# Memory operands beside the state space output, memory tiles ahead of the rows, and the second keys in two halves

## The chip, the cores and the metric

One core of one Trainium2 chip. The metric is device time of one execution in microseconds. Three runs of the kernel before gave 1411.87, 1414.42 and 1416.46 us, a median of 1414.42.

## What is computed

One layer of a streaming encoder on 1024 frames of width 1024, in fp32: token mixing (an S5 state space branch and a forgetting-attention branch, FoX, side by side), cross-attention into 256 memory tokens, and a SwiGLU FFN, each with a norm before, a norm behind and a residual. What the change touches:

```python
# state space branch
g = gelu(y);  out = g * sigmoid(g @ glu_w + glu_b)       # glu
# FoX: 8 heads x 64, causal, blocks of 128 queries
s = q @ k.T * scale + bias;  o = softmax(s) @ v
h = concat(norm(out), norm(o)) @ w_out                    # out_ssm, then the rows
x = x + norm(h)
# memory cross-attention: 4 heads x 256
kv = norm(mem) @ wkv                                      # 256 x 2048, 16 memory tiles
s = (norm(x) @ wq) @ k.T / 16;  x = x + norm(softmax(s) @ v @ wo)
```

The kernel never forms q of the cross-attention. It multiplies the memory keys of a head into wq, and the memory values into wo. These two weight-sized products are called keys (`build_a`) and value weights (`value_weights`) here.

## The kernel before

Every matmul operand is held as two fp32r parts, a high one and the rest. `split` (L111) makes them: ScalarE writes the high half (L113), then VectorE subtracts it from the source for the low half (L115, or L117 where a gain is multiplied in). `mm3` (L121) issues three matmuls: high by high (L122), high by low (L123), low by high (L124). `load_w` (L154) loads a weight tile from SyncE's queue into one of two raw buffers, or into the buffer e, and splits it into one of three buffers `whl`. A raw buffer is free for the next load when its low half is made, a `whl` buffer when its last matmul is through.

Large tiles come from tagged buffers (L193): two a, two b, three c, one d, one e, three t2, two yt. Long-lived operands lie in 16 slabs. Products of TensorE go to four g banks, FoX scores to two s tiles of two banks, and from the end of FoX on the rows to four x banks in their place.

The order of the stages around the change:

1. `in_proj` (L869) runs the input projection. The v tiles (24 matmuls of 128x256 each) are a generator, `v1`, and the tuple `V1_AT` says how many of them are issued ahead of each step of the state space output `ssm_out` (L635), whose first step waits for T_d slabs from DRAM.
2. `fox` (L705) yields one step for each head and block of 128 queries: scores (L730, L731 and the mask L733), the reduction L737 on VectorE, the exp L739 on ScalarE, L740 and L741, some steps later the transposes L758 with evacuations L761 or L763, and every second block the values L772. `paced` (L887) runs 1.02 steps of `fillers` beside each FoX step.
3. `fillers` (L975): the v tiles that are left, `glu` (products of 12 matmuls of 128x512, tanh L681, add L682, multiply L683, split L684, square L688 and sum L689), one step of `out_ssm` (L818, 12 matmuls of 128x256 each, evacuation L836, store L840), then the memory operand (`mem_load`, L950: load, multiply by the row norm L959, split), with a row step after each part, 16 memory tiles (`mem_tile`, L965: weights, 24 matmuls, evacuation L971, store L972), the other rows, and the keys of head 0 and 1, `build_a(0)`. `glu_stats` (L695) makes the row norm of the branch, which the first rows wait for.
4. The rows (L1056 to L1082): for each block of 128 rows two products x of 12 matmuls of 128x512, added to the out_ssm part that comes back from DRAM (L1063 and L1070), squares L1072, a multiplication on GpSimd L1074, the norm, and L1078. Value weights of head 0 and 1 are put between them.
5. At the end (L1231): all keys of head 2 and 3 (`build_a(1)`, 96 matmuls of 128x256), value weights of head 2 (24 of 128x512), the norm of the first cross-attention block `xa_prep(0)`, value weights of head 3, the transposes `xa_turn(0)`, `xa_prep(1)`, and the scores `xa_scores`.

The operands of keys use the buffers e and a for head 0 and 1 and b and a for head 2 and 3 (`("ea", "ba")`). Value weights of the four heads use b, e, e, b. Within an engine the instructions run in the order in which they were issued. A scheduler that runs when the kernel is built decides that order from the code's, so the two can differ by some rows.

Of the kernel before, what the change touches and what calls it, by code (L numbers as in the profile page):

```python
# [13 lines left out]
ALU = mybir.AluOpType  # L14
# [3 lines left out]
P = 128  # L18
# [19 lines left out]
V1_AT = (2, 1, 1, 1, 1)  # L38
# [14 lines left out]
def layer(ctx: ExitStack, tc: tile.TileContext, a, out):  # L53
# [641 lines left out]
    def glu_stats():  # L695
        (sv, acc), = ys_stat
        token_sums(sv, acc)
        tables("natural_log_exp_and_others")
        rsqrt_mean(r_s, sv, 512, 4 * EPS)
# [118 lines left out]
    def out_ssm(ys):  # L818
        for cc in range(4):
            wh, wl = load_w(a["w_out_s"][cc], 256, stage="e" if cc == 2 else None)  # L820
            for j0 in range(0, NT, 2):
                o = t2t([P, 2, 256])
                made = []
                for j in range(j0, j0 + 2):
# [4 lines left out]
                    made.append((j, ps))  # L829
                    if cc + j0 == 0:  # L830
                        yield
                        if j == 0:
                            continue
                        glu_stats()
                    for jj, ps in made:
                        act.activation(out=o[:, jj - j0], in_=ps, func=AF.Copy, scale=r_s[:, jj:jj + 1])  # L836
                    made = []
# [30 lines left out]

    def in_proj():  # L869
# [15 lines left out]
        drain(go)  # L885

# [63 lines left out]
    def mem_load(r, out):  # L950
        rb = row_bcast(r, 2)
        yield
        mh, ml = slab([P, KT, 256]), slab([P, KT, 256])
        for k in range(0, KT, 4):
            m = raw([P, 4, 256])
            sp.dma_start(out=m, in_=a["memT"].rearrange("(k p) m -> p k m", p=P)[:, k:k + 4])
            for kk in range(4):
                with behind():
                    dve.tensor_tensor(out=m[:, kk], in0=m[:, kk], in1=rb, op=ALU.mult)  # L959
                    split(mh[:, k + kk], ml[:, k + kk], m[:, kk], g_mem[:, k + kk:k + kk + 1])  # L960
                if kk % 2:
                    yield
        out.extend((mh, ml))

# [10 lines left out]
    def fillers():  # L975
        yield from v1
        yield from glu(ys)
        mem = []
        rows = out_ssm(ys)
        step(rows)  # L980
        yield
        for _ in mem_load(r_mem[0], mem):
            step(rows)
            yield
        for i in range(16):
            mem_tile(i, *mem)
            yield
        yield from rows
        yield from build_a(0)
# [241 lines left out]
    drain(build_a(1))  # L1231
    for h in range(2, XH):
        if h == 3:
            xa_prep(0)
        drain(value_weights(h))
    xa_turn(0)
    xa_prep(1)
# [390 lines left out]
```

## Time and profile before

| | |
|---|---|
| median of three runs | 1414.42 us |
| the profiled execution | 1412.68 us |
| its span, first to last instruction | 1410.8 us |
| mean granted TensorE clock | 0.993 |
| busy: TensorE, VectorE, ScalarE, GpSimd | 1379.8, 950.5, 652.5, 384.9 us |
| matmuls | 7353 |

The time of an execution has 1.9 us around the span. A row of the timeline gives the start, the duration, engine and line, what is written from what, and in brackets the pause of the engine ahead of it with what ended it. A row of a window gives its length, the busy time and the number of instructions of each engine, the granted TensorE clock (1.00 is full speed) and the DMA share.

### The profile page before, as it was taken

To read this page: it belongs to the slowest core of one execution; us is meant where nothing else is said; L and a number is where in the kernel's file an instruction comes from. 1 tells how busy PE (TensorE), PEld (TensorE's weight loads), DVE (VectorE), ACT (ScalarE), POOL (GpSimd) and SP (SyncE) were. 2 spreads that over 40 slices of the span, in tenths; PEclk is the share of its full clock that TensorE was granted. 3 is DMA by queue.
4 is the path that set the end of the run, shared out by engine and by line. 5 is a ranking of instruction groups with operands and counts; after the bars stand their busy time and mean duration, and the time that the engine had idled before them with its cause. 6 is when DMAs were issued, how large, how long until landed. Compare 5 with 4: busy or idle time off the path is not lost.

```text
span 1410.8 us, 20277 instructions
## 1 busy us (share of the span) xinstructions
PE 1379.8 (98%) x7353; PEld 1162.4 (82%) x7353; DVE 950.5 (67%) x1719; ACT 652.5 (46%) x1289; POOL 384.9 (27%) x430
## 2 busy tenths in 40 slices
PE   9999999999999998999999999999999999999997
PEld 7889888789888786888888788888888888888886
DVE  7949954857666778545467777777776676655566
ACT  7383345766566646433344533333333334544351
POOL 0011110011111142001021376776666662000021
PEclk9999999999999999999999999999999999999999
DMA  6325665357662765024467245554444446955544
GB/s 217 90 106 163 205 224 135 90 165 224 187 180 90 223 203 168 12 83 157 149 212 250 101 171 199 185 174 167 142 160 151 163 150 237 352 201 194 179 165 164
DMA packets 104501, 239.45 MB, mean 170 GB/s; under 512 B 11464, under 2 KB 40136, under 8 KB 104272
## 3 DMA queue, kind: packets, MB, share of 16 engines
q1 hardware_dynamic: 85872, 176.24, 39.6%
q0 software_dynamic: 18528, 61.91, 12.3%
q8 instruction: 58, 0.95, 0.3%
q14 instruction: 43, 0.35, 0.1%
HBM read 169.43 MB, written 77.33 MB: 175 GB/s over the span
## 4 chain that ended last, share of the span: by engine, by line
PE 60%; DVE 0%; ACT 0%; issue 0%; DVEq 0%
PE x L1293 17%; PE g L1293 13%; PE x L1556 7%; PE g L1556 7%; PE g L124 2%; PE g L122 2%; PE g L123 2%; PE x L124 2%; PE x L122 2%; PE x L123 2%; PE g L1090 1%; PE g L1201 1%; DVE whl L115 0%; DVE c L1078 0%; DVE x L1536 0%
## 5 line engine op out<-in xcount | busy, mean ns | idle before, releaser
L1293 PE MATMUL x<-slab,op 128*128 128x512 f32 x984 | 233.2, 389 | 0.5 <-DVE op L115 0.5
L1293 PEld LDWEIGHTS x<-slab,op 128*128 128x128 f32 x984 | 184.6, 188 | 39.3 <-DVE op L115 1.0
L1293 PE MATMUL g<-slab,op 128*128 128x512 f32 x744 | 178.7, 389 | 0.0
L115 DVE TENSOR_TENSOR slab<-slab 128x1024 fp32r<-128x1024 f32 (+2 forms) x92 | 110.2, 1207 | 87.3 <-ACT slab L113 85.5
L1293 PEld LDWEIGHTS g<-slab,op 128*128 128x128 f32 x744 | 139.6, 188 | 29.0
L122 PE MATMUL g<-slab,whl 128*128 128x512 f32 (+1 forms) x416 | 152.2, 366 | 0.8 <-ACT slab L485 0.4
L124 PE MATMUL g<-slab,whl 128*128 128x512 f32 (+1 forms) x416 | 149.1, 359 | 0.0
L123 PE MATMUL g<-slab,whl 128*128 128x512 f32 (+1 forms) x416 | 148.8, 358 | 0.0
L113 ACT ACTIVATE slab<-slab 128x1024 fp32r<-128x1024 f32 (+2 forms) x92 | 94.8, 1036 | 105.9 <-DMA slab<-hs_d 81.1
L1556 PE MATMUL g<-slab 128*128 128x512 f32 x462 | 126.6, 389 | 0.0
L1556 PE MATMUL x<-slab 128*128 128x512 f32 x462 | 126.6, 389 | 0.0
L1556 PEld LDWEIGHTS x<-slab 128*128 128x128 f32 x462 | 86.7, 188 | 18.0
L1556 PEld LDWEIGHTS g<-slab 128*128 128x128 f32 x462 | 86.7, 188 | 18.0
L1369 POOL TENSOR_TENSOR wt<-wt 128x256 f32<-128x256 f32 x88 | 85.9, 976 | 18.6 <-DMA wt<-in_w_down 15.2
L115 DVE TENSOR_TENSOR op<-slab,op 128x512 fp32r<-128x512 f32 x80 | 81.3, 1026 | 11.6 <-ACT op L113 11.3
L122 PEld LDWEIGHTS g<-slab,whl 128*128 128x128 f32 x416 | 78.9, 190 | 12.1 <-ACT whl L113 0.6
L124 PEld LDWEIGHTS g<-slab,whl 128*128 128x128 f32 x416 | 78.7, 189 | 11.8 <-DVE whl L115 0.2
L123 PEld LDWEIGHTS g<-slab,whl 128*128 128x128 f32 x416 | 78.9, 190 | 10.8
L122 PE MATMUL g<-whl,slab 128*128 128x256 f32 (+2 forms) x288 | 85.9, 307 | 1.8 <-ACT yt L318 0.7
L113 ACT ACTIVATE op<-slab 128x512 fp32r<-128x512 f32 x80 | 50.0, 628 | 81.1 <-PE x L1293 38.3
L123 PE MATMUL g<-whl,slab 128*128 128x256 f32 (+2 forms) x288 | 85.7, 298 | 0.0
L124 PE MATMUL g<-whl,slab 128*128 128x256 f32 (+2 forms) x288 | 85.5, 297 | 0.0
(397 smaller groups left out, 2889.7 us busy)
## 6 DMA issues: line engine op xcount, KB each, us to landing
hs_d<-ev POOLq DMA_DIRECT2D x77, 256.0 KB, 2.7
slab<-hs_d SPq DMA_DIRECT2D x35, 512.0 KB
wt<-in_w_down SPq DMA_DIRECT2D x44, 256.0 KB
wt_d<-wt POOLq DMA_DIRECT2D x22, 512.0 KB, 5.1
slab<-in_w_gate SPq DMA_DIRECT2D x20, 512.0 KB
slab<-in_w_up SPq DMA_DIRECT2D x20, 512.0 KB
slab<-wt_d SPq DMA_DIRECT2D x20, 512.0 KB
wd_d<-in_w_down SPq DMA_DIRECT2D x33, 256.0 KB
```

Source lines behind the costliest of these rows:

```text
L113: first = act.activation(out=hi, in_=src, func=AF.Copy, scale=1.0 if mul is None else mul)
L115: (lo_eng or dve).tensor_tensor(out=lo, in0=src, in1=hi.bitcast(F32), op=ALU.subtract)
L122: pe.matmul(ps, lh, rh, start=first, stop=False)
L123: pe.matmul(ps, lh, rl, start=False, stop=False)
L124: pe.matmul(ps, ll, rh, start=False, stop=last)
L1090: pe.transpose(tp[:, k], src[:, (k0 + k) * P:(k0 + k + 1) * P], ident)
L1201: turned = pe.transpose(tp[:, k], h3[:, (4 * n + k) * P:(4 * n + k + 1) * P], ident)
L1293: pe.matmul(ps, x[:, k], y[:, k], start=first and k + n == 0, stop=k == 3 and n == 2, skip_group_check=not first)
L1369: pool.tensor_tensor(out=o, in0=x, in1=y, op=ALU.subtract)
L1556: pe.matmul(banks[n][j], xo[:, u, js], wo[:, v], start=ends[0] and k == 0, stop=ends[1] and k == 2, skip_group_check=onto is not None)
```

## The change

There are four edits.

1. `V1_AT` begins with 3 instead of 2: one more v tile is issued ahead of the first step of `ssm_out`, and one less is left for the fillers.
2. The memory operand is made at the end of `in_proj`, behind the state space output. `mem_load` makes its own broadcast of the row norm (two transposes and an evacuation into yt), and loads the memory in two halves through the single buffer e instead of the raw buffers.
3. `fillers` runs the v tiles, the glu, the 16 memory tiles with `glu_stats` after the first, then all rows of `out_ssm`, then `build_a(0)`. The fillers have 65 steps instead of 67. `out_ssm` loses the code that held back its first two evacuations.
4. At the end value weights of head 2 come first, then the keys of head 2 alone (four steps of `build_a(1)`), `xa_prep(0)`, value weights of head 3, `xa_turn(0)`, and then the keys of head 3.

```diff
-V1_AT = (2, 1, 1, 1, 1)
+V1_AT = (3, 1, 1, 1, 1)
...
                 o = t2t([P, 2, 256])
-                made = []
                 for j in range(j0, j0 + 2):
...
-                    made.append((j, ps))
-                    if cc + j0 == 0:
-                        yield
-                        if j == 0:
-                            continue
-                        glu_stats()
-                    for jj, ps in made:
-                        act.activation(out=o[:, jj - j0], in_=ps, func=AF.Copy, scale=r_s[:, jj:jj + 1])
-                    made = []
+                    act.activation(out=o[:, j - j0], in_=ps, func=AF.Copy, scale=r_s[:, j:j + 1])
...
+    mem = []
+
+    def mem_load(r):
+        rb = tt("yt", [P, 2 * P])
+        ps = g_ps([P, 2 * P])
+        for j in range(2):
+            pe.transpose(ps[:, j * P:(j + 1) * P], r[:, j:j + 1].broadcast_to([P, P]), ident)
+        act.activation(out=rb, in_=ps, func=AF.Copy)
+        mem.extend((slab([P, KT, 256]), slab([P, KT, 256])))
+        for k in range(0, KT, 4):
+            m = tt("e", [P, 4, 256])
+            sp.dma_start(out=m, in_=a["memT"].rearrange("(k p) m -> p k m", p=P)[:, k:k + 4])
+            for kk in range(4):
+                dve.tensor_tensor(out=m[:, kk], in0=m[:, kk], in1=rb, op=ALU.mult)
+                split(mem[0][:, k + kk], mem[1][:, k + kk], m[:, kk], g_mem[:, k + kk:k + kk + 1])
...
         drain(go)
+        mem_load(r_mem[0])
...
-    def mem_load(r, out):
-        rb = row_bcast(r, 2)
-        yield
-        mh, ml = slab([P, KT, 256]), slab([P, KT, 256])
-        for k in range(0, KT, 4):
-            m = raw([P, 4, 256])
-            sp.dma_start(out=m, in_=a["memT"].rearrange("(k p) m -> p k m", p=P)[:, k:k + 4])
-            for kk in range(4):
-                with behind():
-                    dve.tensor_tensor(out=m[:, kk], in0=m[:, kk], in1=rb, op=ALU.mult)
-                    split(mh[:, k + kk], ml[:, k + kk], m[:, kk], g_mem[:, k + kk:k + kk + 1])
-                if kk % 2:
-                    yield
-        out.extend((mh, ml))
...
         yield from glu(ys)
-        mem = []
-        rows = out_ssm(ys)
-        step(rows)
-        yield
-        for _ in mem_load(r_mem[0], mem):
-            step(rows)
-            yield
         for i in range(16):
             mem_tile(i, *mem)
+            if i == 0:
+                glu_stats()
             yield
-        yield from rows
+        yield from out_ssm(ys)
         yield from build_a(0)
...
-    drain(build_a(1))
-    for h in range(2, XH):
-        if h == 3:
-            xa_prep(0)
-        drain(value_weights(h))
+    keys = build_a(1)
+    drain(value_weights(2))
+    step(keys, KT // 2)
+    xa_prep(0)
+    drain(value_weights(3))
     xa_turn(0)
+    drain(keys)
     xa_prep(1)
```

What this does to the order is shown at two places. The first is ScalarE at the end of the glu. In before, behind the tanh of the last glu product (L681, t2_2706 from the bank g_2693), stand the split of an earlier product, square, exp and evacuations, then the broadcast of the memory's row norm (L175) and the first splits of the memory operand (slab_2798 from raw_2800).

```order
L681 ACTIVATE t2_2706<-g_2693,glub_100 128x512
L739 ACTIVATE c_2752,nlr_2753<-c_2752,nlr_2753 128x512
L113 ACTIVATE slab_2640<-t2_2655,gains_98 128x512
L688 ACTIVATE t2_2654<-t2_2655 128x512
L763 ACTIVATE slab_2725<-g_2726 128x128
L763 ACTIVATE slab_2725<-g_2758 128x2x128
L739 ACTIVATE c_2786,nlr_2787<-c_2786,nlr_2787 128x640
L175 ACTIVATE t2_2762<-g_2763 128x256
L763 ACTIVATE slab_2792<-g_2793 128x3x128
L113 ACTIVATE slab_2798<-raw_2800,gains_98 128x256 x2
```

In the changed kernel the last glu product is g_2698 and its tanh writes t2_2711. whl_2818 and whl_2865 are weights of the second and third memory tile.

```order
L113 ACTIVATE whl_2818<-raw_2817 128x1024
L113 ACTIVATE slab_2565<-t2_2623,gains_98 128x512
L688 ACTIVATE t2_2622<-t2_2623 128x512
L113 ACTIVATE whl_2865<-e_2864 128x1024
L681 ACTIVATE t2_2711<-g_2698,glub_100 128x512
L113 ACTIVATE slab_2653<-t2_2668,gains_98 128x512
L688 ACTIVATE t2_2667<-t2_2668 128x512
L763 ACTIVATE slab_2686<-g_2687 128x4x128
```

The splits of the memory operand have gone, and two weight splits stand ahead of the last tanh.

The second place is the end of the rows. On TensorE, in before, the last value weights of head 1 (operands whl_5664 and e_5655) are followed by keys of head 2 from the operand b_5913:

```order
L124 MATMUL g_5802<-whl_5664,e_5655 128x512
L122 MATMUL g_5926<-b_5913,whl_5917 128x256
L123 MATMUL g_5926<-b_5913,whl_5917 128x256
L124 MATMUL g_5926<-b_5913,whl_5917 128x256
L122 MATMUL g_5926<-b_5913,whl_5922 128x256
```

In the changed kernel value weights of head 2 follow, from the operand e_5909. L122 and L123 read its high half, L124 its low half:

```order
L124 MATMUL g_5802<-whl_5664,e_5655 128x512
L122 MATMUL g_5924<-whl_5913,e_5909 128x512
L123 MATMUL g_5924<-whl_5913,e_5909 128x512
L122 MATMUL g_5925<-whl_5913,e_5909 128x512
L123 MATMUL g_5925<-whl_5913,e_5909 128x512
L122 MATMUL g_5942<-whl_5913,e_5909 128x512
L123 MATMUL g_5942<-whl_5913,e_5909 128x512
L122 MATMUL g_5943<-whl_5913,e_5909 128x512
L123 MATMUL g_5943<-whl_5913,e_5909 128x512
L124 MATMUL g_5924<-whl_5913,e_5909 128x512
```

On ScalarE the same four splits stand at this place in both kernels, between the same squares of the rows. In before:

```order
L1072 ACTIVATE yt_5862,ss4_5843<-a_5840 128x256
L113 ACTIVATE a_5996<-t2_5994 128x512
L113 ACTIVATE whl_6000<-raw_5999 128x1024
L113 ACTIVATE slab_5669<-g_5802 128x512
L113 ACTIVATE e_6079<-t2_6077 128x512
L1072 ACTIVATE yt_5882,ss4_5843<-a_5840 128x256
```

In the changed kernel:

```order
L1060 ACTIVATE yt_5862,ss4_5843<-a_5840 128x256
L113 ACTIVATE a_6129<-t2_6127 128x512
L113 ACTIVATE whl_5970<-raw_5969 128x1024
L113 ACTIVATE slab_5669<-g_5802 128x512
L113 ACTIVATE e_5909<-t2_5907 128x512
L1060 ACTIVATE yt_5882,ss4_5843<-a_5840 128x256
```

The operand e keeps its row on ScalarE, behind that of head 3's keys (a). On TensorE its first use has moved from behind the keys to ahead of them.

## The prediction

> **What bounds the kernel now.** I read the page first, then windows of the stretches that the change touches, then the timeline of each engine inside them.
>
> ```profile
> PE 1379.8 (98%) x7353; PEld 1162.4 (82%) x7353; DVE 950.5 (67%) x1719; ACT 652.5 (46%) x1289; POOL 384.9 (27%) x430
> ...
> PE 60%; DVE 0%; ACT 0%; issue 0%; DVEq 0%
> ...
> core 0: us, PE busy (x) PEld busy (x) DVE busy (x) ACT busy (x) POOL busy (x), PEclk, DMA share, GB/s
> ...
> 230.00:246.00 16.00, 14.82 (x68) 11.71 (x68) 12.16 (x33) 10.17 (x24) 0.50 (x1) 0.89 0.42 116
> 270.00:292.00 22.00, 17.43 (x103) 14.29 (x101) 16.50 (x41) 15.96 (x33) 1.45 (x2) 0.77 0.37 109
> 450.00:485.00 35.00, 31.87 (x236) 26.08 (x236) 28.20 (x56) 23.36 (x48) 4.06 (x4) 1.00 0.64 195
> ...
> 538.00:559.00 21.00, 14.10 (x91) 12.65 (x90) 18.80 (x34) 14.15 (x38) 4.92 (x4) 0.92 0.61 187
> ```
>
> TensorE is busy for 98% of the span and the chain that ended last is its own. The change leaves the number and shape of its matmuls as they are, so time can only come from its pauses and from the clock granted behind them. In the four windows the pauses (length less PE busy) are 1.18, 4.57, 3.13 and 6.90 us. What the clock takes is about busy time times one less PEclk: 1.6, 4.0, 0 and 1.1. The stretches therefore lose 2.8, 8.6, 3.1 and 8.0 us. These are the start of the fillers (230), the end of the glu (270), the end of the FoX steps (450) and the keys of head 2 and 3 (538). The change can win 22.5 us there at most, and any of it can be lost again at the new places.
>
> **The change, part by part.**
>
> *One more v tile ahead of ssm_out.*
>
> ```profile
> 189.16 0.46 PE L643 MATMUL g<-slab 128*128 128x128 f32 x2 [1.05 <-DMA slab<-T_d]
> ...
> 538.93 0.28 PE L122 MATMUL g<-b,whl 128*128 128x256 f32 x1
> 539.05 0.28 PE L123 MATMUL g<-b,whl 128*128 128x256 f32 x1
> ```
>
> A 128x256 matmul takes 0.12 us of PE (the distance of the two starts), so a v tile of 24 is 2.9 us, put ahead of a wait of 1.05 us for the T_d slab. It covers that wait: **-1.05** (0 if the load starts later by as much).
>
> *Start of the fillers.* One v tile less is left for the FoX steps, so the first glu product meets the first scores. Its tanh and split, the splits of the second half of the memory operand and a table load stand in the queues of ScalarE and VectorE between the first reductions and exps.
>
> ```profile
> 232.46 0.61 PE L730 MATMUL s<-slab,a 128*128 128x512 f32 x1 [0.90 <-DVE nlr L737]
> ...
> 265.52 0.69 ACT L681 ACTIVATE t<-g,glub 128x512 f32<-128x512 f32 x1 [0.80 <-PE g L124]
> ...
> 272.76 1.28 ACT L152 ACT_TABLE_LOAD   x1
> ```
>
> TensorE waits for exactly that chain there already (0.90 us for L737). The price lies between 0, if the moved product's own 2.75 us of matmuls covers it, and 1.28 + 0.69 = 2.0. I take **+1.2**: the chain has no slack, since PE waits in it now.
>
> *End of the glu.* Eight multiplications and splits of the memory operand leave VectorE here, and out_ssm's first evacuation is no longer waited for. In their place stand the weights of the memory tiles.
>
> ```profile
> 275.24 0.50 PE L730 MATMUL s<-slab,a 128*128 128x512 f32 x1 [1.99 <-DVE nlr L737]
> ...
> 277.30 1.87 PE L237 MATMUL g<-ones,d 128*128 128x1 f32 x8 [0.79 <-DVE d L689]
> ...
> 285.74 0.33 PE L758 MATMUL g<-ident,c 128*128 128x128 f32 x1 [1.50 <-ACT t L836]
> ...
> 272.55 1.76 DVE L959 TENSOR_TENSOR raw<-raw,t 128x256 f32<-128x256 f32 x5
> ...
> 271.49 0.69 DVE L683 SCALAR_TENSOR_TENSOR t<-t,t 128x512 f32<-128x512 f32 x1
> ...
> 283.24 1.06 ACT L113 ACTIVATE whl<-raw 128x1024 fp32r<-128x1024 f32 x1 [2.06 <-DMA raw<-in_wkv]
> ```
>
> The three waits go. But by the new order two splits of memory weights (1.06 each) stand ahead of the tanh of the last glu product, and the second can't start before that product's last matmuls, since it takes their buffer. Counted from the product's end: second split 1.0, then the square sum behind a low half of 1.2 on VectorE, then the tanh: about 2.9 us, in which PE has 0.85 us of transposes and scores. It pauses 2.05. The next scores wait for the second low half (1.2), L683 (0.69) and a reduction of 0.55, less 0.35 and what runs beside: 1.8. Then 0.5 for an evacuation ahead of memory tile 0. That is 4.35 us of pause against 4.57; for the clock I take 2.5 (1.5 to 3.5) against 4.0, since the pauses now lie together and full tiles follow. So 6.85 against 8.6: **-1.7**. If the weights are out of the way in time it is -6; if the clock stays low as long as now, about +1.
>
> *End of the FoX steps.* The out_ssm rows come last and build_a(0) keeps its place at the end, two steps earlier.
>
> ```profile
> 458.65 0.87 PE L772 MATMUL g<-slab 128*64 128x256 f32 x8 [0.99 <-ACT slab L763]
> ...
> 457.23 0.63 ACT L113 ACTIVATE b<-t 128x512 fp32r<-128x512 f32 x1 [3.04 <-DMA t<-kv_d]
> ...
> 486.00 1.06 ACT L113 ACTIVATE whl<-raw 128x1024 fp32r<-128x1024 f32 x1 [1.98 <-DMA raw<-in_wo]
> ```
>
> The split of b that holds ScalarE for 3.04 us until its load has landed stands again ahead of an evacuation, and wo weights follow the out weights through the same two raw buffers. PE has 22 row matmuls now in one piece to cover that. I take **0**, with -1.5 (half of the pauses) to +3 (wo weights 3 us too late).
>
> *Keys and value weights.* This is the largest term. All of the next rows are of before.
>
> ```profile
> 538.48 0.39 PE L123 MATMUL g<-whl,e 128*128 128x512 f32 x1
> 538.71 0.39 PE L124 MATMUL g<-whl,e 128*128 128x512 f32 x1
> ...
> 540.93 0.39 PE L124 MATMUL g<-b,whl 128*128 128x256 f32 x1 [1.25 <-DVE whl L115]
> ...
> 544.70 0.39 PE L122 MATMUL g<-b,whl 128*128 128x256 f32 x1 [1.24 <-DVE slab L115]
> ...
> 548.18 0.39 PE L122 MATMUL g<-b,whl 128*128 128x256 f32 x1 [1.78 <-DVE slab L115]
> ...
> 551.25 0.39 PE L122 MATMUL g<-a,whl 128*128 128x256 f32 x1 [1.36 <-DVE slab L117]
> ...
> 554.03 0.58 PE L124 MATMUL g<-a,whl 128*128 128x256 f32 x1 [1.23 <-DVE whl L115]
> ...
> 544.08 0.63 ACT L113 ACTIVATE a<-t 128x512 fp32r<-128x512 f32 x1 [0.84 <-DVE c L1078]
> 544.62 1.04 ACT L113 ACTIVATE whl<-raw 128x1024 fp32r<-128x1024 f32 x1
> ...
> 546.04 0.62 ACT L113 ACTIVATE e<-t 128x512 fp32r<-128x512 f32 x1
> ...
> 548.05 1.31 DVE L115 TENSOR_TENSOR e<-t,e 128x512 fp32r<-128x512 f32 x1
> ```
>
> Now, from 538.93 on, PE has keys whose operand b was split long before, and works between waits. After the change the first product is value weights, whose operand is e. There is one e buffer, and value weights of head 1 hold it until 538.9. On ScalarE and VectorE the splits of e keep their rows: behind the row norms, the split of a (which waits for L1078 to free a) and a weight split. So the high half of e is done at 546.04 + 0.62 = 546.7 and the low half at 548.05 + 1.31 = 549.4, and PE stands from 538.9 to 546.7. Then eight matmuls of 128x512 need only the high half: 1.8 us at 0.23 each, up to 3.6 at half the clock. The other 16 start between 549.4 and 550.3 and take 3.7 to about 4.5. The product ends near 554, 15.1 us after 538.9, for 5.5 us of work: 9.6 lost. Bounds: 8.6 if the clock holds; 11.5 if it stays at half until 553.
>
> Behind it I count 0.6 for the weights of head 3's values, whose split (1.06) can start only when the last keys' matmuls have freed their buffer. The last keys lie beside the first cross-attention scores, 24 matmuls of 128x512, which need no keys of head 3: no wait. The five waits of before go, with the 8.0 of the window. And five row matmuls (5 x 0.23 = 1.1) that now stand behind the statistics product L237 come ahead of it, so the row work, which starts from it, ends that much later. 9.6 + 0.6 + 1.1 - 8.0 = **+3.3** (+0.8 to +5.5).
>
> The row at 554.03 shows 0.58 instead of 0.39 after two waits of 1.36 and 1.23: here the clock falls after short pauses. The Trainium skill ("TensorE: Matmul & The Clock Gate", Part 1: The HAM clock gate) has half rate after an idle window of about 3.4 us and full rate again after about as much sustained work; by that page as an estimate the stand of 7.8 us would cost 1.7 us of the following work, a loss of 10.3 and a sum 0.7 us higher. The trace agrees that the clock falls, not that it needs so long a pause.
>
> **The sum.** -1.05 + 1.2 - 1.7 + 0 + 3.3 = +1.75 us on the span of 1410.8: 1412.55. The profiled execution has 1.9 us around its span (1412.68 in all) and lies 1.74 under the median of the three runs. With both: 1412.55 + 1.9 + 1.74 = **1416.2 us**. About 0.3%, 4.2 us, is what a measurement of this kernel can tell from no change, so the likeliest is no change that can be told.
>
> **The rivals.**
>
> *The glu end clears (faster).* If the weights of the memory tiles are split before the last glu product needs the queues, the pauses of 2.05 and 1.8 and their clock go: -6 there, and with the keys at their lower bound -1.05 + 0.5 - 6 + 0 + 0.8 = -5.75: 1408.7 us. For it: VectorE loses 8 multiplications and 8 splits between 270 and 290. Against: both splits stand ahead of the tanh in one queue, and the second waits for the product itself. Chance 0.25.
>
> *The stand ahead of e grows (slower).* The split of e hangs on the row chain, and that on loads of row tiles.
>
> ```profile
> 524.15 1.41 DVE L1070 SCALAR_TENSOR_TENSOR a<-x,r_f,a 128x512 f32<-128x512 f32 x2 [1.96 <-DMA a<-t_d]
> ```
>
> It waited 1.96 us for one of them. In before such a delay is partly absorbed by keys that don't need e; in after it goes straight to PE. If the chain ends 4 us later, or the clock stays at half through the product and the queue is 2 us late, this term is +7.3 and the sum +5.75: 1420.2 us. It decides from 2.5 us beyond my 9.6. For it: nothing else is left for PE at that place. Against: most of the chain after 538 is VectorE back to back, whose length is known. Chance 0.30.
>
> *The early keys cover more (no change, lower).* If e were split earlier than a, since a waits for L1078 and e does not, the stand would shrink to a few us and the sum to about -2: 1412.4. The queues are in order and the split of a is ahead: 0.10, of the forecast's 0.45.
>
> **How the numbers follow.** Forecast 0.45 (1410.2 to 1418.6), faster 0.25, slower 0.30. All lower bounds together would be 1406.7, all upper ones 1425.9; they don't fall together. From the cases the range is 1408 to 1423, with 0.2 left outside.
>
> **What would show it.** After the change: no wait at L643 for T_d; PE waiting about 2 us for the tanh (a glu bank) and about 2 for L737 at the end of the glu, with splits of memory weights ahead of them; full tiles after that; one wait of 7 to 9 us for the high half of e ahead of the first value weights matmul; no wait of keys for L117; scores between the last keys. The prediction is wrong if that wait is under 4 us or over 11, if the glu end loses under 3 us, or if PE pauses over 5 us in the last FoX steps.

## The result and the profile after

The changed kernel takes 1420.7 us (median of 6 runs, 1418.94 to 1423.3); beside it the kernel before took 1412.99 us (6 runs). The ratio is 1.0058, with a 95% interval of 1.0038 to 1.0079: 8.2 us slower, between 5.4 and 11.2. The forecast was 1416.2 us with a range of 1408 to 1423, and no change that can be told as the likeliest case. The time lies in the range, but the likeliest case did not come: the change is slower, by the amount of the rival in which the stand ahead of e grows (1420.2). Below, "+5.7" and the like are microseconds against the kernel before, from the ratio of the runs that were made together.

The page of the changed kernel, the busy time of each engine:

```profile
PE 1383.1 (97%) x7353; PEld 1163.3 (82%) x7353; DVE 950.2 (67%) x1719; ACT 654.5 (46%) x1290; POOL 377.8 (27%) x430
```

The profiled execution took 1421.04 us with a span of 1419.3, 8.5 longer than before's. TensorE is busy for 3.3 us more, with the same 7353 matmuls, so they ran at a lower clock, and it pauses for 5.2 us more (36.2 against 31.0). The windows say where. First the kernel before (length, busy time and instructions of PE, PEld, DVE, ACT and POOL, then the granted clock):

```profile
185.00:232.00 47.00, 43.81 (x365) 42.25 (x363) 14.91 (x24) 21.95 (x38) 5.93 (x11) 1.00 0.70 211
232.00:250.00 18.00, 17.54 (x81) 14.24 (x81) 13.60 (x33) 11.68 (x24) 0.00 (x0) 0.91 0.25 78
...
262.00:290.00 28.00, 23.43 (x140) 20.07 (x141) 22.59 (x56) 21.05 (x47) 0.72 (x1) 0.83 0.25 72
450.00:500.00 50.00, 46.87 (x319) 38.39 (x319) 37.14 (x72) 30.72 (x67) 5.03 (x6) 1.00 0.64 201
500.00:542.60 42.60, 41.35 (x192) 34.39 (x191) 32.23 (x55) 20.55 (x73) 24.15 (x19) 1.00 0.69 206
542.60:560.00 17.40, 11.74 (x78) 10.68 (x77) 15.59 (x28) 11.35 (x30) 3.10 (x2) 0.90 0.54 177
```

Then the changed kernel:

```profile
185.00:232.00 47.00, 44.87 (x367) 43.34 (x366) 17.12 (x27) 22.46 (x39) 5.94 (x11) 1.00 0.66 207
232.00:250.00 18.00, 14.99 (x71) 11.73 (x69) 14.28 (x38) 12.99 (x26) 0.00 (x0) 0.91 0.57 163
...
262.00:290.00 28.00, 24.62 (x172) 22.43 (x172) 19.84 (x40) 18.85 (x35) 1.63 (x3) 0.88 0.47 130
450.00:500.00 50.00, 46.56 (x295) 36.63 (x295) 31.72 (x66) 27.07 (x55) 3.71 (x4) 0.93 0.64 180
500.00:542.60 42.60, 41.75 (x182) 33.48 (x180) 29.64 (x51) 17.87 (x68) 20.80 (x17) 1.00 0.62 190
542.60:560.00 17.40, 6.47 (x17) 5.07 (x17) 14.48 (x22) 9.55 (x28) 5.71 (x4) 0.61 0.55 183
```

As in the prediction, the loss of a stretch is its pauses (length less PE busy) plus busy time times one less the clock:

| stretch | before | after | difference | forecast |
|---|---|---|---|---|
| 185 to 250, v tiles and start of the fillers | 3.2 + 2.0 | 2.1 + 4.4 | +1.3 | +0.15 (-1.05 and +1.2) |
| 262 to 290, end of the glu | 8.6 | 6.3 | -2.2 | -1.7 |
| 450 to 500, end of the FoX steps | 3.1 | 6.7 | +3.6 | 0 (-1.5 to +3) |
| 500 to 560, rows, keys, value weights | 1.2 + 6.8 | 0.9 + 13.5 | +6.2 | +3.3 (+0.8 to +5.5) |

The sum is +8.8 (1.26 - 2.22 + 3.57 + 6.22) for 8.5 us of span. The pauses themselves, TensorE's rows in the changed kernel:

```profile
196.62 0.49 PE L643 MATMUL g<-slab 128*128 128x128 f32 x2 [0.83 <-ACT t L316]
...
234.41 0.44 PE L730 MATMUL s<-slab,a 128*128 128x384 f32 x1 [1.52 <-DVE nlr L737]
...
269.17 0.76 PE L758 MATMUL g<-ident,c 128*128 128x128 f32 x4 [2.05 <-ACT t L681]
271.27 0.79 PE L730 MATMUL s<-slab,a 128*128 128x512 f32 x1 [1.33 <-DVE nlr L737]
...
553.54 0.79 PE L122 MATMUL g<-whl,e 128*128 128x512 f32 x1 [10.93 <-ACT e L113]
```

The wait for T_d at L643 is gone, and another stands in its place, for the evacuation at L316 (0.83). The glu end pauses where the forecast put it, 2.05 us for the tanh L681 and then for the reduction. The value weights at the end wait 10.93 us for the high half of e, 3.1 more than the 7.8 of the forecast. After a stand of that length 512-column matmuls follow each other by 0.43 instead of 0.23 us, and the clock of the window is 0.61.

Why e is late shows on VectorE. Lines have moved: L1058, L1064 and L1066 are now the add, the sum of squares and the write of the c tile (L1070, L1076, L1078 before). VectorE before, r_f (with which all rows start) and then the norm of the fourth row tile, which stands ahead of the add at 524.15 that the prediction shows:

```profile
496.76 0.17 DVE L145 SCALAR_TENSOR_TENSOR r_f<-rst,rsy 128x8 f32<-128x8 f32 x1
...
520.10 0.16 DVE L1076 TENSOR_REDUCE ss<-ss 128x1 f32<-128x4 f32 x1 [0.52 <-ACT yt L1072]
...
522.03 0.16 DVE L145 SCALAR_TENSOR_TENSOR r<-rst,rsy 128x1 f32<-128x1 f32 x1
```

VectorE in the changed kernel:

```profile
500.13 0.17 DVE L145 SCALAR_TENSOR_TENSOR r_f<-rst,rsy 128x8 f32<-128x8 f32 x1
...
526.81 0.75 DVE L1058 SCALAR_TENSOR_TENSOR a<-x,r_f,a 128x512 f32<-128x512 f32 x1 [5.29 <-DMA a<-t_d]
527.48 0.15 DVE L1064 TENSOR_REDUCE ss<-ss 128x1 f32<-128x4 f32 x1
...
530.21 0.16 DVE L145 SCALAR_TENSOR_TENSOR r<-rst,rsy 128x1 f32<-128x1 f32 x1
```

The chain that ended last, in the changed kernel (start, time, what):

```profile
515.82 0.27 SPq L1051
...
516.13 10.56 DMA a<-t_d
...
526.81 0.75 DVE a L1058
```

The first add of the fifth row tile now stands one row ahead of the norm of the fourth. It waits for a load that lands at 526.7, and the norm waits behind it; nothing else holds the norm, since L1064 starts as soon as the add is over (527.48). The load itself is not late: it lands 26.6 us after r_f, and in before the add at 524.15 starts 27.4 us after it. What is late is the norm: its r comes at 530.2, 30.1 us after r_f, against 25.3 before. The last row of that norm (L1066) frees the buffer of the next row loads; they start when it ends, 34.3 us after r_f against 31.6 in before, so what follows is late. From r_f to the split of e there are 52.7 us (500.13 to the row at 552.87 below), and 49.3 in before (496.76 to 546.04). ScalarE in the changed kernel:

```profile
552.87 0.62 ACT L113 ACTIVATE e<-t 128x512 fp32r<-128x512 f32 x1
```

No edit touches those lines. The scheduler that fixes each engine's order placed them so; no run shows why it ranks them otherwise. VectorE's order around that place, the lines of before on the left:

```
before                                    after
L1070 a<-x,r_f,a x2  (fourth tile)        L1058 a<-x,r_f,a x2  (fourth tile)
L115  b<-t,b                              L115  b<-t,b
L1076 ss (fourth tile)                    L1058 a<-x,r_f,a     (fifth tile)
L139, L141, L145                          L1064 ss (fourth tile)
L1070 a<-x,r_f,a x2  (fifth tile)         L139, L141, L145
                                          L1058 a<-x,r_f,a     (fifth tile)
```

### The profile page after: what moved, and what is told of

Same layout as the page of the kernel before. It is cut to its first block, busy times and chain, and to the rows that moved or that the text cites. A ratio compares the mean times of both kernels' runs of the same rounds, so it can differ in the third digit from the quotient of the medians.

```text
span 1419.3 us, 20286 instructions
## 1 busy us (share of the span) xinstructions
PE 1383.1 (97%) x7353; PEld 1163.3 (82%) x7353; DVE 950.2 (67%) x1719; ACT 654.5 (46%) x1290; POOL 377.8 (27%) x430
## 4 chain that ended last, share of the span: by engine, by line
PE 85%; issue 6%; DVE 3%; DMA 2%; ACT 2%; POOL 1%; SPq 0%; DVEq 0%; POOLq 0%; ACTq 0%
PE x L1282 17%; PE g L1282 13%; PE g L122 7%; PE x L1545 7%; PE g L1545 7%; PE g L124 7%; PE g L123 7%; PE x L122 2%; PE x L123 2%; PE x L124 2%; PE g L758 2%; PE g L772 2%; PE s L730 1%; PE s L731 1%; PE g L1078 1%
## 5 line engine op out<-in xcount | busy, mean ns | idle before, releaser
L122 PE MATMUL g<-slab,whl 128*128 128x512 f32 (+1 forms) x416 | 153.1, 368 | 0.8 <-ACT slab L485 0.4
L123 PE MATMUL g<-slab,whl 128*128 128x512 f32 (+1 forms) x416 | 149.7, 360 | 0.0
L124 PE MATMUL g<-slab,whl 128*128 128x512 f32 (+1 forms) x416 | 149.5, 360 | 0.0
L115 DVE TENSOR_TENSOR op<-slab,op 128x512 fp32r<-128x512 f32 x80 | 84.9, 1072 | 10.7 <-ACT op L113 10.4
L1358 POOL TENSOR_TENSOR wt<-wt 128x256 f32<-128x256 f32 x88 | 82.9, 942 | 26.9 <-DMA wt<-in_w_down 23.5
L122 PEld LDWEIGHTS g<-slab,whl 128*128 128x128 f32 x416 | 79.9, 192 | 12.0 <-ACT whl L113 0.6
L124 PEld LDWEIGHTS g<-slab,whl 128*128 128x128 f32 x416 | 79.6, 191 | 11.8 <-DVE whl L115 0.2
L123 PEld LDWEIGHTS g<-slab,whl 128*128 128x128 f32 x416 | 79.9, 192 | 10.7
L113 ACT ACTIVATE op<-slab 128x512 fp32r<-128x512 f32 x80 | 49.9, 628 | 80.8 <-PE x L1282 38.5
L122 PE MATMUL g<-whl,slab 128*128 128x256 f32 (+2 forms) x288 | 85.1, 304 | 1.5 <-ACT yt L318 0.7
L124 PE MATMUL g<-whl,slab 128*128 128x256 f32 (+2 forms) x288 | 84.9, 295 | 0.0
L123 PE MATMUL g<-whl,slab 128*128 128x256 f32 (+2 forms) x288 | 84.8, 294 | 0.0
```

Source lines behind the costliest of these rows:

```text
L113: first = act.activation(out=hi, in_=src, func=AF.Copy, scale=1.0 if mul is None else mul)
L115: (lo_eng or dve).tensor_tensor(out=lo, in0=src, in1=hi.bitcast(F32), op=ALU.subtract)
L122: pe.matmul(ps, lh, rh, start=first, stop=False)
L123: pe.matmul(ps, lh, rl, start=False, stop=False)
L124: pe.matmul(ps, ll, rh, start=False, stop=last)
L1358: pool.tensor_tensor(out=o, in0=x, in1=y, op=ALU.subtract)
```

## The experiments

The theory after this trace: three losses, each with its own cause. The end of the FoX steps (row products and out weights all behind the last transposes), the swap of add and norm on VectorE, and the wait for the one e buffer. The rivals: that one of them makes up the whole, or that edit 4 alone does, as the prediction had it.

**1. The end as before, in the changed kernel.** Edits 1 to 3 stay.

```diff
-    keys = build_a(1)
-    drain(value_weights(2))
-    step(keys, KT // 2)
-    xa_prep(0)
-    drain(value_weights(3))
+    drain(build_a(1))
+    for h in range(2, XH):
+        if h == 3:
+            xa_prep(0)
+        drain(value_weights(h))
...
-    drain(keys)
```

> The changed kernel with the end of before (all keys of head 2 and 3, then both value weights); the other three edits stay. Theory (the stretches add up): the account of the two traces puts 5.5 us on the keys and value weights and 0.85 on the rows ahead of them, so this kernel is 1.5 to 3.5 us slower than before, and the wait for the high half of e is gone. Rival (the fillers' order is the cause, and the late rows would hold up keys as much as value weights): 6 us or more slower than before, with over 11 us lost between the end of the rows and the cross-attention.

1419.43 us, ratio 1.0040 (1.0025 to 1.0056): +5.7, nearer the rival. Taking edit 4 away wins only 2.5 us back. Its add, too, stands ahead of the norm. So most of the loss is not edit 4's own. Without edit 4 the late row chain meets the keys: TensorE waits 3.53 us for the split of their weights:

```profile
544.05 0.58 PE L122 MATMUL g<-b,whl 128*128 128x256 f32 x1 [3.53 <-ACT whl L113]
```

**2. The new end alone.** The kernel before with edit 4 (the same lines the other way).

> Before with the new order of keys and value weights alone. Theory (the wait is set by the split of e, which hangs on the row chain): a single wait of 7 to 9 us for the high half of e, and 2 to 4 us slower than before. Rival (the wait is long only because the new FoX end makes the rows late): a wait of under 4 us, and no slower than before by more than 1 us.

1414.29 us, ratio 1.0007 (0.9995 to 1.0019): +1.0. TensorE in this kernel:

```profile
549.87 0.79 PE L122 MATMUL g<-whl,e 128*128 128x512 f32 x1 [8.22 <-ACT e L113]
```

The wait is about as long as forecast (7.8), with add and norm in the order of before. Its price is less than the 2 to 4 expected and than the forecast's +3.3, near the forecast's lower bound of 0.8. The order is not the only thing that can make the chain late: the add waits 3.40 us here in place of 1.96, and the split of e starts 51.4 us after r_f (549.20 and 497.83) against 49.3 in before.

**3. The values of head 2 and 3 in b, in the changed kernel.** The keys of head 2 take e in turn.

```diff
-            kh = tt(("ea", "ba")[c][h], [P, 2, 2, 256], F32R)
+            kh = tt(("ea", "ea")[c][h], [P, 2, 2, 256], F32R)
...
-        vh = tt("beeb"[h], [P, 2, 2, 256], F32R)
+        vh = tt("bebb"[h], [P, 2, 2, 256], F32R)
```

> The changed kernel with two buffers exchanged: value weights of head 2 take their operand from b and keys of head 2 from e; every engine keeps the order of its instructions. Theory (e is the cause): the wait of 10.9 us goes, what is left there are waits for evacuations and weights of 2 to 5 us in all, and the kernel is 6 to 10 us faster than the changed one, so between 1 us slower and 2 us faster than before. Rival (value weights first wait anyway, for banks and weights that come out of the same queues): over 8 us still lost there, 5 us or more slower than before.

1417.23 us, ratio 1.0026 (1.0010 to 1.0042): +3.7, 4.5 less than the changed kernel, under the 6 to 10 expected. TensorE in this kernel:

```profile
546.54 0.50 PE L122 MATMUL g<-whl,b 128*128 128x512 f32 x1 [2.56 <-ACT whl L113]
548.42 0.79 PE L123 MATMUL g<-whl,b 128*128 128x512 f32 x1 [1.38 <-DVE whl L115]
```

The wait for e is gone, and the weights' split is late next: it stands in the same queues behind the same row chain. The orders are not wholly kept, as the expectation has it: on TensorE the low-half products of the first value weights no longer stand behind the high-half ones, and behind the split of e some rows of VectorE and ScalarE move. So the 4.5 us are for the buffer with these shifts.

**4. Other pace of the fillers.** The changed kernel with 0.99 instead of 1.02 steps beside a FoX step. The fillers then last to the end of FoX, and add and norm stand as before.

```diff
-RATE = 1.02
+RATE = 0.99
```

> The changed kernel with fillers paced at 0.99 instead of 1.02, so that its 65 steps end with the FoX steps as the 67 of before did. Theory (the FoX end lost 3.2 us because the fillers run out two steps early, which puts the row products and their weights behind the last transposes): the waits for slab and whl at the first row products go, 2 to 4 us faster than the changed kernel, 4 to 6 us slower than before. Rival (the FoX end loses time whatever the pace, by the loads of the out weights): within 1 us of the changed kernel.

1416.04 us, ratio 1.0010 (0.9995 to 1.0025): +1.4, or 6.8 less than the changed kernel, where 2 to 4 less was expected. The wait for e is 7.51 us. This one number undoes two things together, the end of the FoX steps and the swap.

**5. Only the swap undone.** The pace stays at 1.02; the first add of the fifth tile is held behind the norm of the fourth.

```diff
-            dve.scalar_tensor_tensor(out=t[:, hs], in0=ps, scalar=r_f[:, j:j + 1], in1=t[:, hs], op0=ALU.mult, op1=ALU.add)
+            with (tc.issue_after(norm[1].ins) if (n, h) == (4, 0) else ExitStack()):
+                dve.scalar_tensor_tensor(out=t[:, hs], in0=ps, scalar=r_f[:, j:j + 1], in1=t[:, hs], op0=ALU.mult, op1=ALU.add)
...
-        rsqrt_mean(r, ss, D)
+        norm = rsqrt_mean(r, ss, D)
```

> The changed kernel with one pair of rows exchanged on VectorE, as they stood in before: the norm of the row tile a_5561 ahead of the add L1058 of the next tile, a_5624 (which waits for its load), and the two squares that follow on ScalarE. Theory (this row is why the wait for e grew from the forecast 8.9 to 10.9 us: the add waits 5.3 us for a load with the norm, the store and the next loads behind it): the wait for the high half of e is 7 to 9 us, 2 to 4 us faster than the changed kernel, 4 to 6 us slower than before. Rival (the loads themselves are late, so the chain is late whatever stands first): the wait stays over 10 us, within 1 us of the changed kernel.

1416.09 us, ratio 1.0021 (1.0012 to 1.0030): +3.0, 5.2 less than the changed kernel. VectorE and ScalarE, then TensorE in this kernel:

```profile
502.92 0.17 DVE L145 SCALAR_TENSOR_TENSOR r_f<-rst,rsy 128x8 f32<-128x8 f32 x1
...
529.80 1.41 DVE L1059 SCALAR_TENSOR_TENSOR a<-x,r_f,a 128x512 f32<-128x512 f32 x2 [2.54 <-DMA a<-t_d]
...
551.50 0.62 ACT L113 ACTIVATE e<-t 128x512 fp32r<-128x512 f32 x1
```

```profile
552.17 0.80 PE L122 MATMUL g<-whl,e 128*128 128x512 f32 x1 [7.67 <-ACT e L113]
```

One row put back where it was in before: VectorE's wait falls from 5.29 to 2.54, from r_f to the split of e takes 48.6 us instead of 52.7, and TensorE's wait falls from 10.93 to 7.67. This is more than the 2 to 4 us expected, and the rival falls. The swap is a cause of the loss in this kernel. Whether its 5.2 us or the 4.5 of the third experiment weigh more can't be told: the 8.2 from which both are counted has an interval of about 3 us to either side.

**6. Pace 0.99 and values in b together** (edits 3 and 4 of this list).

> The changed kernel with both mends: fillers at pace 0.99, and value weights of head 2 in the buffer b with keys of head 2 in e. Theory (the pace and the wait for e are two separate losses, 6.8 and about 4 us): 2 to 5 us faster than the kernel at 0.99, so 1 to 4 us faster than before. Rival (with the rows on time the value weights wait as long for banks and weights as they did for e): within 1 us of the kernel at 0.99.

1411.96 us, ratio 0.9986 (0.9977 to 0.9995): -2.0, faster than both kernels, and 3.4 less than at pace 0.99 alone, as the theory has it.

**7. Pace 0.99 and the end as before** (edits 1 and 4 of this list).

> The first three edits at pace 0.99, with the end of before. Theory (edits 1 to 3 gain nothing at any pace: what the glu end saves, the start of the fillers loses; and the new order of the keys costs about 1 us): 0.5 us faster to 1 us slower than before. Rival (edits 1 to 3 are a gain once the fillers fill all FoX steps, and the keys' order eats it): 2 to 4 us faster than before.

1413.84 us, ratio 1.0001 (0.9991 to 1.0011): +0.1. Edits 1 to 3 of the change, with the rows in the old order, neither gain nor lose, to within about 1.5 us.

**8. The third v tile alone.** The kernel before with edit 1.

```diff
-V1_AT = (2, 1, 1, 1, 1)
+V1_AT = (3, 1, 1, 1, 1)
```

> Before with the first edit alone, three v tiles ahead of the state space output. Theory (the wait for T_d goes, but the first step then waits for the evacuation of the v tile, and the first scores meet a glu product): 0 to 2 us slower than before, with a wait at the first L643 of 0.8 to 2.5 us for L316 and over 2.5 us of waits at the first scores. Rival (the v tile covers the wait): 0.5 to 1.5 us faster.

1413.16 us, ratio 0.9994 (0.9980 to 1.0008): -0.8, no change that can be told. TensorE in this kernel, at the place where T_d was waited for:

```profile
198.72 0.80 PE L643 MATMUL g<-slab 128*128 128x128 f32 x2 [3.23 <-ACT t L316]
```

The wait changes its name and not its place. In eight of the nine kernels with three v tiles it is between 0.83 (changed kernel) and 3.23 us (here), against 1.05 to 1.63 for T_d in those with two; the kernel of the seventh has no such wait. The other half of the expectation fell: there is no wait at the first scores here, where over 2.5 us were expected.

This kernel also has the swap, from the first edit alone: VectorE's first add of the fifth tile (526.45) stands ahead of the sum of the fourth (527.11), and the first add of the fourth, which waits 5.80 us for its load, stands inside the norm of the third. VectorE, then ScalarE:

```profile
522.37 0.75 DVE L1070 SCALAR_TENSOR_TENSOR a<-x,r_f,a 128x512 f32<-128x512 f32 x1 [5.80 <-DMA a<-t_d]
...
526.45 0.74 DVE L1070 SCALAR_TENSOR_TENSOR a<-x,r_f,a 128x512 f32<-128x512 f32 x1
527.11 0.14 DVE L1076 TENSOR_REDUCE ss<-ss 128x1 f32<-128x4 f32 x1
```

```profile
550.25 0.62 ACT L113 ACTIVATE e<-t 128x512 fp32r<-128x512 f32 x1
```

It pays nothing for it. Here the fifth tile's add finds its load landed, the norm of the fourth ends ahead of the fifth tile's sum, and the next row loads start 30.1 us after r_f (501.79), earlier than in before (31.6). The split of e comes 48.5 us after r_f, against 49.3 in before. So the order costs by the wait that it puts ahead of other rows, and not by itself.

**9. Swap undone and values in b, pace 1.02** (edits 3 and 5 of this list). What is left of the three losses is the end of the FoX steps.

> The changed kernel at its own rate of 1.02, with both the add of the next row tile put behind the norm of the previous one and the values of head 2 and 3 split into b. The end of the FoX steps keeps the order of the changed kernel: row products and out weights behind the last transposes. Theory (three separate losses: end of FoX steps about 3.3 us, order of the row adds about 4 to 5, wait for e about 4 to 5): with two of the three taken away the kernel lies 2 us below to 1.5 us above the kernel before, above the run at rate 0.99 with values in b (2.0 us below) by 1 to 3 us. Rival (the end of the FoX steps costs nothing by itself and only the order of the row adds and the wait for e count): within 0.7 us of that run, 1.3 to 2.7 us below the kernel before. Rival (losses overlap, so that one edit takes most of both): 2 us or more above.

1412.36 us, ratio 0.9986 (0.9973 to 0.9999): -2.0, the same as at pace 0.99. The time is the first rival's, and the theory falls in this part: the end of the FoX steps costs nothing that can be told, though two intervals of 1.3 and 1.9 us to either side can't exclude the 1 us with which the theory began. The windows of this stretch in this kernel, and in the third and the fifth experiment, all with the pace of the changed kernel:

```profile
450.00:500.00 50.00, 46.73 (x310) 37.57 (x310) 32.76 (x69) 27.84 (x56) 3.70 (x4) 1.00 0.64 178
```

```profile
450.00:500.00 50.00, 46.60 (x315) 37.39 (x315) 33.53 (x70) 29.10 (x60) 3.85 (x5) 1.00 0.64 181
```

```profile
450.00:500.00 50.00, 46.48 (x322) 37.52 (x321) 33.41 (x69) 29.52 (x59) 4.43 (x5) 1.00 0.65 178
```

They pause for 3.3 to 3.5 us, as the changed kernel does (3.4), and as before does (3.1). The other 3.3 of the changed kernel's 6.7 came from a clock of 0.93 that none of the three shows; the eighth experiment's window has 0.93 too. But the changed kernel's six executions have a median (1420.7) as long as its profiled one, so the others lose as much in all, and no trace shows where.

**10. The swap alone, in the kernel before.** The norm of the fourth tile is issued behind the first add of the fifth. Its second add is held behind that norm, as in the changed kernel. Some rows behind them move as well: the last row of the fourth norm stands ahead of the sum of the fifth tile, and the next add moves up by some rows.

```diff
-            dve.scalar_tensor_tensor(out=t[:, hs], in0=ps, scalar=r_f[:, j:j + 1], in1=t[:, hs], op0=ALU.mult, op1=ALU.add)
+            with (tc.issue_after(done[1].ins) if (n, h) == (4, 1) else ExitStack()):
+                add = dve.scalar_tensor_tensor(out=t[:, hs], in0=ps, scalar=r_f[:, j:j + 1], in1=t[:, hs], op0=ALU.mult, op1=ALU.add)
+            if (n, h) == (4, 0):
+                with tc.issue_after(add.ins):
+                    done = late()
...
+        def norm(ss=ss, ss4=ss4, r=r, t=t, xt=xt, j=j):
...
+        if n == 3:
+            late = norm
+        else:
+            norm()
```

> The kernel before with one thing changed: the norm of the fourth row tile is issued behind the first add of the fifth, on VectorE, as it stands in the changed kernel (the norm's two ScalarE rows and its store move with it). End of the FoX steps, keys and value weights as before. Theory (the add waits for its load with the norm behind it, and the delay passes down the row chain to the end): 3 to 5 us slower than the kernel before, VectorE waiting 3 us or more for that load, and TensorE standing that much longer between the row products and the first scores. Rival (the swap alone is absorbed, since the keys of before don't need e): within 1.2 us of the kernel before.

1416.01 us, ratio 1.0018 (1.0006 to 1.0030): +2.5, between the two and nearer the theory. VectorE, then ScalarE in this kernel:

```profile
525.32 0.75 DVE L1071 SCALAR_TENSOR_TENSOR a<-x,r_f,a 128x512 f32<-128x512 f32 x1 [5.68 <-DMA a<-t_d]
```

```profile
548.91 0.62 ACT L113 ACTIVATE e<-t 128x512 fp32r<-128x512 f32 x1
```

The wait of 5.68 us in place of 1.96 is there, and the split of e comes 2.87 us later than in before (546.04). With the old end about half of the swap's price stays: 2.5 (0.8 to 4.2) of the 5.2 that undoing it won in the changed kernel.

Over all kernels the split of e starts 48.6 to 49.9 us after r_f with add and norm in the order of before, except for the second (51.4) and the twelfth (51.1) experiment, and 52.2 to 53.0 us with the swap, except for the eighth (48.5).

**11. The new end with values in b, in the kernel before** (edit 4 of the change, edit 3 of this list).

> The kernel before with the new order of keys and value weights at the end, and values of head 2 and 3 split into b, keys into e and a. Theory (the new end costs a stand of 8 us for e in place of the 8 us of the old waits, and without that stand it gains): 1.5 to 4 us faster than the kernel before, no wait for e ahead of the first value weights, under 4 us of pause left there. Rival (the row chain sets the end whatever the order of the products, as the row chain is what all of them wait for): within 1.2 us of the kernel before.

1410.87 us, ratio 0.9982 (0.9969 to 0.9994): -2.5, as the theory has it; against the second experiment (+1.0) the buffer is worth 3.5. TensorE in this kernel:

```profile
538.88 0.50 PE L123 MATMUL g<-whl,b 128*128 128x512 f32 x1 [0.43 <-DVE whl L115]
542.75 0.57 PE L122 MATMUL g<-whl,b 128*128 128x512 f32 x1 [2.43 <-DVE slab L115]
546.23 0.80 PE L122 MATMUL g<-whl,b 128*128 128x512 f32 x1 [0.78 <-DVE slab L115]
```

3.6 us of pauses in place of one of 8.22. This is what edit 4 can gain when its first operand has a buffer of its own.

**12. Pace 0.99, values in b, two v tiles as in before.** Edit 1 of the change is taken back; the hold of the fifth experiment is in, since the scheduler swaps add and norm again without it.

> The changed kernel at rate 0.99 with values in b, and two v tiles ahead of the state space output as in the kernel before in place of three (the norm is kept ahead of the next add by hand, since the scheduler's order falls back otherwise). Theory (the third v tile gains nothing: the wait for T_d turns into one for the evacuation at L316, and the fillers' start loses 1.5 us for it): the same or 1 to 2 us faster than the run at rate 0.99 with values in b, so 2 to 4 us below the kernel before. Rival (the v tile gains its 1.05 us): about 1 us slower than that run, 1 us below the kernel before.

1408.56 us, ratio 0.9970 (0.9955 to 0.9984): -4.2, just beyond the theory's 2 to 4, and the fastest of all kernels here. The window of the glu end in this kernel:

```profile
262.00:290.00 28.00, 28.00 (x216) 25.15 (x215) 23.96 (x50) 23.34 (x46) 2.16 (x4) 1.00 0.53 159
```

No pause, full clock: the 6.3 us of the changed kernel are gone here. With one v tile more among the fillers the steps fall so that products stand beside the last tanh. Against the sixth experiment this is 2.2 us, but the intervals touch, and the order of other rows moved as well. So the gain is shown for the whole kernel, not for the v tile alone. Some of it is lost again at the end of the FoX steps, where TensorE pauses 5.0 us between 450 and 500 against 3.1 in the sixth.

## Why the prediction was right and wrong

- **The v tile ahead of ssm_out (-1.05).** Too large. The T_d wait went, and a wait for L316 came, so about 0.6 was left of it: before's pause ahead of 232.46 (0.90) lies with 0.44 in the first window, 3.19 - 0.44 = 2.75 against 2.13. By the eighth experiment the edit alone is worth nothing that can be told.
- **Start of the fillers (+1.2).** Right in place, low in size: TensorE waits 1.52 us for L737 where it waited 0.90. The stretch from 232 to 250 loses 2.3 more, or 1.9 with the 0.44 that belongs to before's; the bound was 2.0. Its reason is shown only in part: with the third v tile alone (eighth experiment) the first scores don't wait at all, and no run tells the glu product apart from the moved memory operand.
- **End of the glu (-1.7).** Right. -2.2 came, with the first pause as worked out (2.05), the second smaller (1.33 for 1.8). The rival that the glu end clears did not come in the changed kernel. The twelfth experiment clears it, but not for the rival's reason: two weight splits (265.05 and 266.26) still stand ahead of the last tanh (267.23).
- **End of the FoX steps (0).** Right in its pauses (3.1 to 3.4). The profiled execution lost 3.3 more to the clock; the same pauses cost no clock in the third, fifth and ninth experiment, so the order of this stretch is not enough to cause it.
- **Keys and value weights (+3.3).** Wrong in size: +6.2, over its upper bound of 5.5. The step that failed is "So the high half of e is done at 546.04 + 0.62 = 546.7". The splits of e did keep their rows, as the prediction said, but it took the time of before for the chain ahead of them. That chain lost its order, with an add ahead of a norm, so the split of e began 52.7 us after r_f and not 49.3. The mechanism, one e buffer and an operand behind the row chain, was right: a wait of 8.22 us in the second experiment for 7.8 forecast. In the changed kernel it was 10.93, over the 7 to 9 expected and just inside the 4 to 11 that the prediction set. Its price was put too high: with edit 4 alone it is +1.0, and undoing the swap takes 5.2 off the changed kernel.
- **The rival in which the stand ahead of e grows (1420.2).** It had the chain 4 us late, and 3.5 came; it put that down to late loads, and the load was on time, with the norm held behind it. That its total fits to 0.5 us is in part luck: the keys lost 6.2 for its 7.3, and the end of the FoX steps 3.6 for its 0.

By the experiments on the changed kernel, 5.2 us hang on the swap (fifth; 5.7 by the third against the ninth) and 4.5 on the wait for e (third; 5.0 by the fifth against the ninth), each to within about 3 us. Both undone take off 10.2, about as much as the two together, and turn the +8.2 into -2.0. The order of the rows was fixed when the kernel was built, and could be read ahead of any run. The prediction read the engines' order for the fillers and the end, and assumed it for the rows between, which no edit touches.

The Trainium skill ("TensorE: Matmul & The Clock Gate", Part 1, Architectural detail) says that ScalarE and VectorE work strictly first in, first out. The trace agrees: the sum of squares L1064 started as soon as an add was over that had waited 5.29 us. What stays open: why the first experiment lost 5.7, when the swap costs 2.5 in the kernel before and edits 1 to 3 cost 0.1 at the other pace. Its trace shows where, between 500 and 560: the stretch loses 12.2 us there, 9.8 in the tenth and 8.1 in before, and the first keys wait 3.53 us for the split of their weights, against 1.32 in the tenth. Why they wait longer no run shows, and the intervals are nearly as wide as those 3.1 us.

## What to carry to other kernels

Where a scheduler sets the order, an edit in one stage can swap rows in a later stage that no line of it touches: the order of every engine on the chain behind the edit is to be read, not assumed, and above all whether a row that waits for a load stands ahead of one that is ready. What it costs depends on that wait: the same pair in the changed order was worth 5.2 us in one kernel, 2.5 in another and nothing in a third. Work put first at the end of a chain needs an operand that doesn't hang on that chain; another buffer turned the new end from +1.0 to -2.5 us. And a loss that one profile shows as clock alone is to be looked for in a second kernel with the same rows, ahead of giving it a cause.

## What the runs showed of the hardware

The granted clock doesn't follow from the pauses alone. At one place the changed kernel paused twice, TensorE's rows:

```profile
487.95 0.73 PE L123 MATMUL x<-slab 128*128 128x512 f32 x1 [0.76 <-DVE slab L115]
488.48 0.63 PE L124 MATMUL x<-slab 128*128 128x512 f32 x1
489.95 0.79 PE L122 MATMUL g<-whl,b 128*128 128x512 f32 x1 [0.84 <-ACT whl L113]
...
494.38 0.63 PE L124 MATMUL g<-whl,b 128*128 128x512 f32 x1
494.80 0.43 PE L123 MATMUL g<-whl,b 128*128 128x512 f32 x1
495.08 0.39 PE L124 MATMUL g<-whl,b 128*128 128x512 f32 x1
```

The ninth experiment paused at the same two places:

```profile
487.35 0.50 PE L123 MATMUL x<-slab 128*128 128x512 f32 x1 [0.15 <-DVE slab L115]
489.50 0.50 PE L122 MATMUL g<-whl,b 128*128 128x512 f32 x1 [1.42 <-ACT whl L113]
...
492.56 0.39 PE L123 MATMUL x<-slab 128*128 128x512 f32 x1
```

1.60 us of pauses against 1.57. In the one execution TensorE ran at half rate from 487.95 to 494.8, for 6.9 us (512-column matmuls 0.43 us apart); in the other at full rate throughout (0.23 us apart). Half rate was there behind the first pause, of 0.76 us: the stretch from 488 to 489 has a clock of 0.52, ahead of the second pause. The ninth experiment kept full rate behind one of 1.42 us. The Trainium skill ("TensorE: Matmul & The Clock Gate", Part 1: The HAM clock gate) has half rate after an idle window of about 3.4 us, and full rate after as much sustained work; it also says that the window runs freely, so that the loss varies from run to run. The traces agree that the loss varies; they don't agree with the length of the pause (0.76 us), and half rate lasted 6.9 us, twice the page's figure. Executions of one kernel spread by about 5 us to either side (before: 1408.5 to 1418.6), so a term of 3 us in one profile can be of that execution alone.
